# Who adds the squares at the fronts of stages, and where the low parts of twelve weight panels come from

## The chip, the cores and the metric

The kernel runs on one core of a Trainium2 chip. The metric is device time in microseconds (us), the median of the runs of one build. The engines are named PE (TensorE, matrix products), DVE (VectorE), ACT (ScalarE), POOL (GpSimd) and SP (SyncE, which issues most DMA transfers).

## What is computed

The reference is two blocks of a transformer in float32 on a sequence of 512 tokens and a width of 1024. Cut to what matters here:

```
def first_block(x, p, ...):
    for i in range(2):
        hn = rmsnorm(h, mix_norm[i])
        if i == 0: h = h + conformer_conv(hn, ...)
        else:      h = h + fox_attention(hn, ..., *shared_kv(h, kv_norm, ...))
        hn = rmsnorm(h, ffn_norm[i])
        h = h + square(relu(hn @ ffn_w1[i])) @ ffn_w2[i]
        gate = sigmoid(rmsnorm(h, ple_norm[i]) @ ple_w_gate[i])
        h = h + gate * (p[i] @ ple_w_proj[i])
    return rmsnorm(h, final_norm)

def second_block(x, mem, ...):
    h = rms_norm(x, mix_norm_gain)
    ... recurrence, block attention, memory attention, gated merge ...
    x = x + merged @ w_out
    h = rms_norm(x, ffn_norm_gain)
    x = x + (gelu(causal_dwconv(h @ w_ffn_gate, ...)) * (h @ w_ffn_up)) @ w_ffn_down
    return rms_norm(x, final_norm_gain)
```

Each `rmsnorm` divides by the root of the mean of squares over the 1024 features. Between the blocks two of them follow each other: the final norm of the first block and the first norm of the second.

## The kernel before

The hidden state `h` is held with features on the partitions: eight tiles of 128 features by 512 tokens. A float32 product is made of three passes on PE with operands rounded to a shorter type (fp32r): every operand is split in a high part, which is the rounded value, and a low part, which is the rest. Activations give `xh` and `xl`, weights `hi` and `lo`, and the passes are `xh*hi`, `xl*hi` and `xh*lo`, one 128x512 matmul each.

The weights come in panels of 128x2048 floats (1 MB), in the fixed order of a list of keys: `("w1", 1, 0, 0)` is the first panel of the first matrix of the second feed-forward layer, `("plg", l, i)` the gate of the per-layer part, `("xa", i)` the first panels of the second block. SP loads a panel into one of two `raw` buffers (`load`, line 299). `splitting` (line 529) then has ACT cast four pieces of 128x512 to `hi`, and DVE subtract them (`lo = raw - hi`, in `part`); panels of three kinds (`LO_POOL`, line 1901) have POOL subtract. Each piece of `hi` and `lo` has two buffers, so that a panel's piece takes the place of the same piece two panels before.

Panels in the set `SEVEN`, which are multiplied by a scheme of seven block products, get three of their low pieces in another way: `lows_by_dma` (line 367) has ACT write `-raw`, rounded, into `lo`, and POOL issue a DMA that reads the same weights from HBM again and adds them to that (line 362). Such a piece may begin when the panel before its own is the one being multiplied.

The order of all instructions is written by a planner, the class `Flow`. It keeps a clock per engine, from costs by operation, and a list of side jobs (generators); each time a matmul is written, the jobs that are due by these clocks take a step, by priority. So an instruction's place on its engine follows from costs and due times, and each engine then runs its own row in order.

A `Front` (line 687) makes the norm in front of a stage. As each of the eight tiles of `h` is finished, ACT writes its split `xh` and its square `sq`, and the squares are added up to one tile by `Norm.add` (line 639): the first square is the sum's start, six additions are POOL's and the last one DVE's. PE then takes the mean (four 1-column matmuls `tp<-C,sq`), DVE and POOL the inverse root, and PE spreads it (`tp<-C,s`). There are eight fronts. The first, at the program's start, uses two sums (`two=True`); the seven others are those before the feed-forward of the first layer (at about 244 us of the span), its per-layer gate (585), the second layer's mixing (633), its feed-forward (887) and its gate (1239), the second block (1286) and the second block's feed-forward (1735). At 1286 us a plain `Norm`, `n2` (line 1514), sums the squares for the final norm of the first block beside the front's own sum (`gg` in these rows is the product of gains by which `xh` is scaled there).

Of the kernel before, what the change touches and what calls it, by code (L numbers as in the profile page):

```python
# [15 lines left out]
S = 512  # L16
D = 1024
KT = 8
# [50 lines left out]
_KEYS = _panel_keys()  # L69
# [3 lines left out]
class Engine:  # L73


    def __init__(self, flow, eng, cost):
        self.flow, self.eng, self.cost, self.t, self.table = flow, eng, cost, 0.0, None
# [37 lines left out]
def _pe_cost(op, out, ins):  # L115
    n, dt = ins[1].free_size(), ins[1].dtype
    if op == "transpose" or (dt == F32 and n == 1):
        return 0.11
    if dt == F32:
        return 0.01 + n * 4 / 2400  # L120
    return max(0.109 if dt == F32R else 0.059, n / 2390)
# [106 lines left out]
def kernel(ctx: ExitStack, tc, gain0, x_t, p_t, mem_t, vec, w, w_f, w_lru, rows, consts, out):  # L228
# [9 lines left out]
    flow = Flow()  # L238
    act, dve = Engine(flow, nc.scalar, _act_cost), Engine(flow, nc.vector, _dve_cost)
    pool, pe = Engine(flow, nc.gpsimd, _pool_cost), Engine(flow, nc.tensor, lambda *a: 0.12 if flow.halves else _pe_cost(*a))  # L240
# [57 lines left out]
    raws, parts, early = {}, {}, {}  # L298

    def load(i, pieces=1):  # L300
        if i < len(_KEYS) and i not in raws:
            if _KEYS[i] in SEVEN:
                early[i] = flow.spawn(lows_by_dma(i), 0.0, 2)
            r = wp.tile([128, PW], F32, name=nm("raw"), tag="raw", bufs=2)
            raws[i] = r
            c = PW // pieces
            return [lambda k=k: dma(r[:, c * k:c * k + c], w[i, :, c * k:c * k + c]) for k in range(pieces)]
        return []

    class Panel:  # L310


        def __init__(self, key):
            self.key, self.blocked = key, key[0] in BLOCKED
            self.q = {}
# [24 lines left out]
    def part(i, k, pieces, low):  # L340

        if i not in parts:
            parts[i] = Panel(_KEYS[i])
        c = PW // pieces
        r = raws[i][:, c * k:c * k + c]
        hi, lo = parts[i].cols(c * k, c)
        gain = GAINED.get(_KEYS[i][0])
        if gain is not None:
            g = col(gain, k)
            act.activation(hi, r, AF.Copy, scale=g)  # L350
            dve.scalar_tensor_tensor(lo, r, g, hi.bitcast(F32), op0=ALU.mult, op1=ALU.subtract)
        else:
            act.copy(hi, r)
            low.tensor_sub(lo, r, hi.bitcast(F32))
# [12 lines left out]
    def lows_by_dma(i):  # L367

        r = raws[i]
        for b in range(3):  # L370
            c = slice(S * b, S * b + S)
            yield lambda: cur[0] >= i - 1 or (i - 2, b) in spent
            yield r[:, c]
            yield flow.quiet(act, patience=HOLD)
            if i not in parts:
                parts[i] = Panel(_KEYS[i])
            lo = parts[i].piece("lo", b)
            act.mul(lo, r[:, c], -1.0)
            yield lo
            accumulate(lo, w[i, :, c])  # L380

    def sums_split(i):
# [13 lines left out]
        pan.s1, pan.s2, pan.s3, pan.s4 = s1, s2, s3, s4  # L396
        wait = lambda e: flow.quiet(e, slack=1.2, patience=HOLD_SUMS)
        yield wait(dve)
# [130 lines left out]
    def splitting(i):  # L529
        if _KEYS[i] in SEVEN:  # L530
            yield from sums_split(i)
            return
        pieces = KT if _KEYS[i][0] in GAINED else 4
        low = pool if _KEYS[i][0] in LO_POOL else dve
        c = PW // pieces
        for k in range(pieces):
            yield raws[i][:, c * k:c * k + c]
            yield flow.quiet(act, low, patience=HOLD)
            part(i, k, pieces, low)

    ahead = {}
# [91 lines left out]
    class Norm:  # L633


        def __init__(self, n=S, total=KT, two=False):
            self.n, self.left, self.two = n, total, two
            self.parts = []

        def add(self, t, g=None):  # L640
            n = self.n
            self.left -= 1
            q = slot(p="sq")
            act.activation(q[:, :n], t, AF.Square, scale=1.0 if g is None else g)
            if len(self.parts) <= self.two:
                self.parts.append(q)
                return
            s = self.parts[self.left % (1 + self.two)]
            (dve if self.left % 2 and self.two or self.left == 0 else pool).tensor_add(s[:, :n], s[:, :n], q[:, :n])
            if self.left == 0 and self.two:  # L650
                dve.tensor_add(s[:, :n], s[:, :n], self.parts[1][:, :n])
            self.sum = s
# [31 lines left out]
    class Front:  # L684


        def __init__(self, g=None, two=False):
            self.g = g
            self.xs = [None] * KT
            self.norm = Norm(two=two)  # L690
            self.r4 = self.rbc = self.side = None

        def add(self, f, t):
# [861 lines left out]
    xa, ga = [None] * 4, [None] * 4  # L1555
# [311 lines left out]
    for n, cut, queues in zip(norms, cuts, ((dma,), (dma, nc.scalar.dma_start))):  # L1867
# [4 lines left out]
        s = flow.spawn(output(n, cut, queues), 0.0, 0)  # L1872
# [19 lines left out]
HOLD = 1.2  # L1892
# [7 lines left out]
MEM_PERIOD = 9.0  # L1900
LO_POOL = ("pw1", "vm", "o")
HOLD_SUMS = 0.3
BLOCKED = ("w1", "gu")
SEVEN = {("w1", l, c, i) for l in range(2) for c in range(1, 4) for i in range(4)}
SEVEN |= {("gu", m) for m in range(8, 24)}
# [156 lines left out]
```

## Time and profile before

| | us |
|---|---|
| median of three runs | 2131.7 |
| lowest and highest run | 2130.28 and 2131.87 |
| profiled execution, its own time | 2132.37 |
| its span on the core | 2129.5 |
| PE busy within the span | 2078.7 |

The span is the time from the first to the last instruction on the core, and 2.9 us lie around it. All windows and start times below count from the span's start. Of PE's 11360 matmuls most have 512 columns; at full clock they follow each other every 0.2265 us (six in a row start at 630.15, 630.37, 630.60, 630.83, 631.05 and 631.28 us). A matmul's own duration is longer than that, since matmuls are pipelined.

### The profile page before, as it was taken

What the parts mean: (1) busy time and instruction counts of PE and PEld (TensorE: products, weight loads), DVE (VectorE), ACT (ScalarE), POOL (GpSimd) and SP (SyncE); (2) the same over time, 40 slices, a digit from 0 to 9 for tenths busy, and PEclk for the clock granted to TensorE, in tenths of its full rate; (3) what the DMA queues carried; (4) which work ended last, traced back from release to release, by engine and by line L of the source; (5) the groups of instructions that cost most, each with busy time, mean ns of one, the idle gap of its engine ahead of it and who ended that gap; (6) DMA issues with size and microseconds to landing.
All of it is one profiled execution on the core that took longest, in us unless ns stands there. A gap on an engine that the chain in (4) does not pass through costs nothing.

```text
span 2129.5 us, 30406 instructions
## 1 busy us (share of the span) xinstructions
PE 2078.7 (98%) x11360; PEld 1783.7 (84%) x11360; DVE 1428.5 (67%) x2534; ACT 1159.2 (54%) x2372; POOL 473.2 (22%) x500
## 2 busy tenths in 40 slices
PE   7999999999999999899999999999999999999998
PEld 6867889899878887789898887878888888899997
DVE  5997557566576887666565677775574557776683
ACT  5776446456445676455464553665462333485672
POOL 4882101101121326401011121331010010020212
PEclk9999999999999999999999999999999999999999
DMA  5215236547322111236455523112222423375661
GB/s 185 99 61 197 88 115 155 129 129 183 115 81 86 61 62 61 70 106 142 125 153 127 170 87 123 62 61 101 99 71 88 139 80 119 112 158 147 148 170 60
DMA packets 58050, 240.73 MB, mean 113 GB/s; under 512 B 6824, under 2 KB 10152, under 8 KB 35504
## 3 DMA queue, kind: packets, MB, share of 16 engines
q1 hardware_dynamic: 40048, 206.81, 28.7%
q0 software_dynamic: 17280, 31.46, 9.1%
q8 instruction: 89, 1.46, 0.3%
q10 hardware_dynamic: 576, 0.52, 0.1%
q14 instruction: 57, 0.47, 0.1%
HBM read 229.00 MB, written 9.77 MB: 112 GB/s over the span
## 4 chain that ended last, share of the span: by engine, by line
PE 78%; DVE 10%; ACT 7%; issue 2%; POOL 2%; DMA 1%; SPq 0%; DVEq 0%; ACTq 0%; POOLq 0%
PE mm L83 69%; PE sc L83 6%; DVE t L83 2%; DVE sc L83 2%; ACT hi L83 2%; PE tp L83 1%; ACT t L83 1%; DVE lo L83 1%; PE ptp L83 1%; DVE xl L83 1%; POOL acc L83 1%; DVE h L83 1%; ACT lo L83 1%; DVE xc L83 1%; ACT sh L83 1%
## 5 line engine op out<-in xcount | busy, mean ns | idle before, releaser
L83 PE MATMUL mm<-xh,hi 128*128 128x512 f32 (+1 forms) x2096 | 797.6, 381 | 8.7 <-ACT hi L83 7.3
L83 PE MATMUL mm<-xh,lo 128*128 128x512 f32 (+1 forms) x2096 | 796.1, 380 | 7.0 <-DVE lo L83 6.6
L83 PE MATMUL mm<-xl,hi 128*128 128x512 f32 (+1 forms) x2096 | 795.4, 379 | 0.0
L83 PEld LDWEIGHTS mm<-xh,hi 128*128 128x128 f32 x2096 | 397.1, 189 | 79.6 <-ACT hi L83 7.6
L83 PEld LDWEIGHTS mm<-xh,lo 128*128 128x128 f32 x2096 | 396.8, 189 | 79.4 <-DVE lo L83 9.1
L83 PEld LDWEIGHTS mm<-xl,hi 128*128 128x128 f32 x2096 | 396.9, 189 | 69.5
L83 ACT CAST hi<-raw 128x512 fp32r<-128x512 f32 x596 | 347.2, 617 | 111.9 <-PE mm L83 96.3
L83 DVE TENSOR_TENSOR lo<-raw,hi 128x512 fp32r<-128x512 f32 x424 | 291.3, 724 | 60.5 <-ACT hi L83 58.6
L362 POOL DMA_DIRECT2D lo<-in_w x120 | 104.0, 866 | 760.5 <-ACT lo L83 699.5
L83 DVE TENSOR_TENSOR h<-mm,h 128x512 f32<-128x512 f32 (+1 forms) x113 | 75.5, 670 | 242.4 <-PE mm L83 242.3
L83 POOL TENSOR_TENSOR sq<-sq,sq 128x512 f32<-128x512 f32 (+1 forms) x69 | 84.5, 1226 | 437.2 <-ACT sq L83 436.6
L83 ACT ACTIVATE lo<-raw 128x512 fp32r<-128x512 f32 x120 | 76.5, 637 | 81.5 <-PE mm L83 81.5
L83 POOL TENSOR_SCALAR P<-P,s 128x128 f32<-128x128 f32 (+2 forms) x112 | 64.2, 578 | 243.4 <-DVE s L83 195.7
L83 DVE TENSOR_TENSOR sl<-sum,sh 128x512 fp32r<-128x512 f32 x120 | 82.4, 686 | 15.6 <-ACT sh L83 14.9
L83 PE MATMUL mm<-ch,sh 128*128 128x256 f32 x320 | 90.6, 283 | 0.0
L83 PE MATMUL mm<-cl,sh 128*128 128x256 f32 x320 | 90.6, 283 | 0.0
L83 PE MATMUL mm<-ch,sl 128*128 128x256 f32 x320 | 90.6, 283 | 0.0
L83 ACT ACTIVATE xh<-h,V 128x512 fp32r<-128x512 f32 x40 | 28.6, 722 | 112.9 <-DVE h L83 112.9
L83 PE MATMUL mm<-ch,hi 128*128 128x256 f32 x352 | 88.0, 285 | 1.6 <-ACT p L83 1.6
L83 ACT CAST sh<-sum 128x512 fp32r<-128x512 f32 x120 | 75.4, 628 | 20.1 <-DVE sum L83 20.1
L83 PE MATMUL mm<-ch,lo 128*128 128x256 f32 x288 | 81.5, 283 | 0.0
L83 POOL TENSOR_TENSOR acc<-acc,tap 128x482 f32<-128x482 f32 (+29 forms) x60 | 77.2, 1286 | 13.1 <-ACT tap L83 9.5
(295 smaller groups left out, 3908.1 us busy)
## 6 DMA issues: line engine op xcount, KB each, us to landing
raw<-in_w SPq DMA_DIRECT2D x175, 1024.0 KB
lo<-in_w POOLq DMA_DIRECT2D x120, 256.0 KB, 5.2
prd<-pr SPq DMA_DIRECT2D x16, 256.0 KB
pr<-prd SPq DMA_DIRECT2D x16, 256.0 KB
h<-in_x_t SPq DMA_DIRECT2D x8, 256.0 KB
resid<-h SPq DMA_DIRECT2D x8, 256.0 KB
h<-resid SPq DMA_DIRECT2D x8, 256.0 KB
out<-out SPq DMA_DIRECT2D x12, 128.0 KB
```

The source lines that it names most:

```text
L83: f(out, *args, **kw)
L362: nc.gpsimd.dma_start(out, src, accum_op=ALU.add)
```

## The change

Two things change. A `Norm` gets a flag `alone`, which all fronts but the first set: DVE then makes all seven additions of squares, so 42 additions go from POOL to DVE. `n2` has no such flag and keeps POOL. And a set `LO_DMA` names twelve panels, two of `w1` of the second layer, the two `xa` and the eight `plg`: their four low pieces come by `lows_by_dma`, ACT's negation and POOL's accumulating DMA, where DVE subtracted. `part` casts their high pieces only, and `splitting` waits for ACT alone there.

```
     def load(i, pieces=1):
         if i < len(_KEYS) and i not in raws:
-            if _KEYS[i] in SEVEN:
+            if _KEYS[i] in SEVEN or _KEYS[i] in LO_DMA:
                 early[i] = flow.spawn(lows_by_dma(i), 0.0, 2)
...
         c = PW // pieces
+        if _KEYS[i] in LO_DMA:
+            act.copy(parts[i].piece("hi", k), raws[i][:, c * k:c * k + c])
+            return
         r = raws[i][:, c * k:c * k + c]
...
     def lows_by_dma(i):
...
-        for b in range(3):
+        for b in range(3 if _KEYS[i] in SEVEN else 4):
...
-            yield flow.quiet(act, low, patience=HOLD)
+            yield flow.quiet(*((act,) if _KEYS[i] in LO_DMA else (act, low)), patience=HOLD)
...
-        def __init__(self, n=S, total=KT, two=False):
-            self.n, self.left, self.two = n, total, two
+        def __init__(self, n=S, total=KT, two=False, alone=False):
+            self.n, self.left, self.two, self.alone = n, total, two, alone
...
-            (dve if self.left % 2 and self.two or self.left == 0 else pool).tensor_add(s[:, :n], s[:, :n], q[:, :n])
+            (dve if self.alone or self.left % 2 and self.two or self.left == 0 else pool).tensor_add(
+                s[:, :n], s[:, :n], q[:, :n])
...
-            self.norm = Norm(two=two)
+            self.norm = Norm(two=two, alone=not two)
...
+LO_DMA = {("w1", 1, 0, 0), ("w1", 1, 0, 1), ("xa", 0), ("xa", 1)} | {("plg", l, i) for l in range(2) for i in range(4)}
```

The instructions of PE stay the same ones. Apart from the seven fronts and the twelve panels, each engine's row keeps its order, but for one load that SP issues earlier, ahead of eight transfers of the attention at about 650 us. What moves is shown at two places.

First ACT, at the front of the second feed-forward (the stretch from 878 to 890 us). `xh` and `sq` come from the eight tiles `h1755` to `h1762`, `raw1896` is panel `("w1", 1, 0, 0)`, `V_74` holds gains. Before:

```order
L83 ACTIVATE xh1921_9002<-h1755_8402,V_74 128x512
L83 ACTIVATE sq1927_9019<-h1755_8402 128x512
L83 ACTIVATE xh1923_9008<-h1756_8404,V_74 128x512
L83 ACTIVATE xh1925_9015<-h1757_8406,V_74 128x512
L83 ACTIVATE sq1933_9038<-h1756_8404 128x512
L83 CAST hi1937_9048<-raw1896_8872 128x512
L83 ACTIVATE xh1929_9027<-h1758_8408,V_74 128x512
L83 ACTIVATE xh1931_9034<-h1759_8410,V_74 128x512
L83 CAST hi1939_9060<-raw1896_8872 128x512
L83 ACTIVATE xh1935_9046<-h1760_8412,V_74 128x512
L83 ACTIVATE sq1941_9070<-h1757_8406 128x512
L83 CAST hi1945_9080<-raw1896_8872 128x512
```

and now:

```order
L83 ACTIVATE lo1921_8996<-raw1896_8888 128x512
L83 ACTIVATE lo1922_8999<-raw1896_8888 128x512
L83 ACTIVATE lo1923_9002<-raw1896_8888 128x512
L83 ACTIVATE lo1924_9005<-raw1896_8888 128x512
L83 ACTIVATE xh1925_9030<-h1755_8418,V_74 128x512
L83 ACTIVATE sq1931_9047<-h1755_8418 128x512
L83 ACTIVATE xh1927_9036<-h1756_8420,V_74 128x512
L83 ACTIVATE xh1929_9043<-h1757_8422,V_74 128x512
L83 ACTIVATE sq1937_9066<-h1756_8420 128x512
L83 CAST hi1941_9076<-raw1896_8888 128x512
L83 ACTIVATE xh1933_9055<-h1758_8424,V_74 128x512
L83 ACTIVATE xh1935_9062<-h1759_8426,V_74 128x512
```

The four negations of the panel stand ahead of the first `xh` of the front; behind them the casts and splits follow in the old order.

On DVE, at the same place, before (`raw1896` as above, `o`, `mm`, `sc` and `tp` results of PE):

```order
L83 SCALAR_TENSOR_TENSOR xl1926_9016<-h1757_8406,V_74,xh1925_9015 128x512
L83 TENSOR_TENSOR lo1938_9049<-raw1896_8872,hi1937_9048 128x512
L83 TENSOR_TENSOR lo1940_9061<-raw1896_8872,hi1939_9060 128x512
L83 SCALAR_TENSOR_TENSOR xl1930_9028<-h1758_8408,V_74,xh1929_9027 128x512
L83 SCALAR_TENSOR_TENSOR xl1932_9035<-h1759_8410,V_74,xh1931_9034 128x512
L83 TENSOR_TENSOR h1761_8414<-mm1934_9043,h1761_8414 128x512
L83 TENSOR_TENSOR lo1946_9081<-raw1896_8872,hi1945_9080 128x512
L83 SCALAR_TENSOR_TENSOR xl1936_9047<-h1760_8412,V_74,xh1935_9046 128x512
L83 TENSOR_TENSOR lo1949_9095<-raw1896_8872,hi1948_9094 128x512
L83 TENSOR_TENSOR h1762_8416<-mm1942_9076,h1762_8416 128x512
L83 SCALAR_TENSOR_TENSOR xl1944_9079<-h1761_8414,V_74,xh1943_9078 128x512
L83 TENSOR_TENSOR lo1959_9133<-raw1928_9024,hi1958_9132 128x512
```

and now:

```order
L83 SCALAR_TENSOR_TENSOR xl1930_9044<-h1757_8422,V_74,xh1929_9043 128x512
L83 SCALAR_TENSOR_TENSOR xl1934_9056<-h1758_8424,V_74,xh1933_9055 128x512
L83 TENSOR_TENSOR sq1931_9047<-sq1931_9047,sq1943_9093 128x512
L83 SCALAR_TENSOR_TENSOR xl1936_9063<-h1759_8426,V_74,xh1935_9062 128x512
L83 TENSOR_TENSOR h1761_8430<-mm1938_9071,h1761_8430 128x512
L83 TENSOR_TENSOR sq1931_9047<-sq1931_9047,sq1948_9112 128x512
L83 SCALAR_TENSOR_TENSOR xl1940_9075<-h1760_8428,V_74,xh1939_9074 128x512
L83 TENSOR_TENSOR sq1931_9047<-sq1931_9047,sq1950_9121 128x512
L83 TENSOR_TENSOR h1762_8432<-mm1944_9099,h1762_8432 128x512
L83 TENSOR_TENSOR sq1931_9047<-sq1931_9047,sq1956_9136 128x512
L83 SCALAR_TENSOR_TENSOR xl1946_9103<-h1761_8430,V_74,xh1945_9102 128x512
L83 TENSOR_TENSOR sq1931_9047<-sq1931_9047,sq1958_9151 128x512
```

The four `lo` subtractions of this panel are gone, and additions to the sum of squares `sq1931` stand between the splits; the tile `h1762` is taken up before four of them are done.

Second POOL, at the entry to the second block (1277 to 1288 us). `sq2602` (now `sq2609`) is the sum of `n2`, `sq2614` (now `sq2618`) the front's own. The last six additions on POOL before:

```order
L83 TENSOR_TENSOR sq2602_12621<-sq2602_12621,sq2644_12797 128x512
L83 TENSOR_TENSOR sq2614_12658<-sq2614_12658,sq2647_12812 128x512
L83 TENSOR_TENSOR sq2602_12621<-sq2602_12621,sq2650_12831 128x512
L83 TENSOR_TENSOR sq2614_12658<-sq2614_12658,sq2657_12851 128x512
L83 TENSOR_TENSOR sq2602_12621<-sq2602_12621,sq2668_12900 128x512
L83 TENSOR_TENSOR sq2614_12658<-sq2614_12658,sq2671_12915 128x512
```

and now, with the DMAs of the low pieces of the last `plg` and the `xa` panels:

```order
L83 TENSOR_TENSOR sq2609_12671<-sq2609_12671,sq2632_12776 128x512
L365 DMA lo2630_12769<-in_w 128x512
L83 TENSOR_TENSOR sq2609_12671<-sq2609_12671,sq2641_12823 128x512
L365 DMA lo2648_12846<-in_w 128x512
L365 DMA lo2649_12852<-in_w 128x512
L365 DMA lo2650_12858<-in_w 128x512
L365 DMA lo2651_12864<-in_w 128x512
L83 TENSOR_TENSOR sq2609_12671<-sq2609_12671,sq2655_12884 128x512
L83 TENSOR_TENSOR sq2609_12671<-sq2609_12671,sq2662_12926 128x512
L365 DMA lo2672_12954<-in_w 128x512
L365 DMA lo2673_12961<-in_w 128x512
```

The front's own additions are gone from POOL, and those of `n2` stand between the DMA issues. On DVE the last additions of that place were

```order
L83 TENSOR_TENSOR t2655_12846<-t2655_12846,pr2509_12160 128x512
L83 TENSOR_TENSOR h1761_8414<-h1761_8414,t2655_12846 128x512
L83 TENSOR_TENSOR t2662_12888<-mm2656_12848,rbc2595_12559 128x512
L83 SCALAR_TENSOR_TENSOR xl2670_12904<-h1761_8414,gg2578_12498,xh2669_12903 128x512
L83 TENSOR_TENSOR t2662_12888<-t2662_12888,pr2510_12162 128x512
L83 TENSOR_TENSOR h1762_8416<-h1762_8416,t2662_12888 128x512
L83 TENSOR_TENSOR lo2673_12928<-raw2642_12792,hi2672_12927 128x512
L83 TENSOR_TENSOR sq2602_12621<-sq2602_12621,sq2674_12933 128x512
L83 TENSOR_TENSOR lo2678_12944<-raw2642_12792,hi2677_12943 128x512
L83 SCALAR_TENSOR_TENSOR xl2676_12937<-h1762_8416,gg2578_12498,xh2675_12936 128x512
L83 TENSOR_TENSOR sq2614_12658<-sq2614_12658,sq2680_12956 128x512
```

and are now

```order
L83 TENSOR_TENSOR t2659_12898<-t2659_12898,pr2509_12184 128x512
L83 TENSOR_TENSOR h1761_8430<-h1761_8430,t2659_12898 128x512
L83 SCALAR_TENSOR_TENSOR xl2664_12930<-h1761_8430,gg2578_12526,xh2663_12929 128x512
L83 TENSOR_TENSOR sq2618_12706<-sq2618_12706,sq2665_12939 128x512
L83 TENSOR_TENSOR t2666_12942<-mm2660_12900,rbc2597_12595 128x512
L83 TENSOR_TENSOR t2666_12942<-t2666_12942,pr2510_12186 128x512
L83 TENSOR_TENSOR h1762_8432<-h1762_8432,t2666_12942 128x512
L83 TENSOR_TENSOR sq2609_12671<-sq2609_12671,sq2679_12993 128x512
L83 SCALAR_TENSOR_TENSOR xl2681_12997<-h1762_8432,gg2578_12526,xh2680_12996 128x512
L83 TENSOR_TENSOR sq2618_12706<-sq2618_12706,sq2684_13016 128x512
```

with no subtraction of a weight panel among them. PE's row has the means of these two sums at other places than before by a few matmuls: at 633 us the mean `tp<-C,sq` stands 8 matmuls later than before, at 887 us 6 later, and at 1286 us that of `n2` 4 later; the other fronts' stand where they stood.

## Rows read from the trace of the kernel before

**Rows 1.** The page: busy time of each engine, share of the span, instructions.

```profile
PE 2078.7 (98%) x11360; PEld 1783.7 (84%) x11360; DVE 1428.5 (67%) x2534; ACT 1159.2 (54%) x2372; POOL 473.2 (22%) x500
```

**Rows 2.** Waits of PE: line waited for, total us, times, longest.

```profile
PE tp L83 <- DVE sq L83: 13.3, 6, 4.2
...
PE mm L83 <- DVE lo L83: 6.6, 1, 6.6
```

**Rows 3.** Busy time by stretch (us) at the fronts, with granted clock and DMA share.

```profile
core 0: us, PE busy (x) PEld busy (x) DVE busy (x) ACT busy (x) POOL busy (x), PEclk, DMA share, GB/s
...
627.00:642.00 15.00, 13.11 (x66) 10.70 (x65) 10.55 (x20) 6.92 (x15) 3.42 (x3) 1.00 0.21 72
...
1281.00:1303.00 22.00, 17.97 (x83) 15.12 (x82) 13.80 (x24) 7.75 (x14) 4.63 (x4) 0.84 0.14 48
330.00:380.00 50.00, 50.00 (x380) 48.31 (x379) 36.30 (x69) 33.04 (x65) 5.72 (x7) 1.00 0.59 149
...
1259.00:1281.00 22.00, 22.00 (x99) 18.22 (x98) 18.70 (x22) 13.33 (x24) 10.70 (x8) 1.00 0.35 120
```

**Rows 4.** Timeline of PE around three stalls: start, us, instruction, [idle before <-releaser].

```profile
635.60 0.58 PE L83 MATMUL tp<-C,sq 128*128 128x1 f32 x4 [1.89 <-DVE sq L83]
...
894.38 0.80 PE L83 MATMUL mm<-xh,lo 128*128 128x512 f32 x1 [6.62 <-DVE lo L83]
...
897.54 0.45 PE L83 MATMUL mm<-xh,hi 128*128 128x512 f32 x1
...
1280.87 0.39 PE L83 MATMUL mm<-xh,lo 128*128 128x512 f32 x1
...
1290.73 1.84 PE L83 MATMUL tp<-C,sq 128*128 128x1 f32 x8 [4.03 <-DVE sq L83]
...
1296.84 1.03 PE L83 MATMUL tp<-C,sq 128*128 128x1 f32 x8
```

**Rows 5.** Timeline of ACT, DVE and POOL at 878 to 895 us.

```profile
878.56 0.72 ACT L83 ACTIVATE xh<-h,V 128x512 fp32r<-128x512 f32 x1 [8.59 <-DVE h L83]
...
886.30 0.61 ACT L83 CAST hi<-raw 128x512 fp32r<-128x512 f32 x1
...
885.86 3.45 DVE L83 SCALAR_TENSOR_TENSOR xl<-h,V,xh 128x512 fp32r<-128x512 f32 x2
...
892.58 1.74 DVE L83 TENSOR_TENSOR lo<-raw,hi 128x512 fp32r<-128x512 f32 x1
...
885.50 8.28 POOL L83 TENSOR_TENSOR sq<-sq,sq 128x512 f32<-128x512 f32 x5 [2.57 <-ACT sq L83]
```

**Rows 6.** Timeline of DVE and ACT at 1283 to 1291 us.

```profile
1283.80 0.69 DVE L83 TENSOR_TENSOR t<-mm,rbc 128x512 f32<-128x512 f32 x1
...
1286.56 1.75 DVE L83 TENSOR_TENSOR t<-t,pr 128x512 f32<-128x512 f32 x1
...
1289.07 0.72 ACT L83 ACTIVATE sq<-h,V 128x512 f32<-128x512 f32 x1 [2.26 <-DVE h L83]
```

**Rows 7.** Timeline of DVE and POOL at 629 to 636 us.

```profile
630.34 1.60 DVE L83 TENSOR_TENSOR t<-t,pr 128x512 f32<-128x512 f32 x1
...
634.77 0.68 DVE L83 TENSOR_TENSOR sq<-sq,sq 128x512 f32<-128x512 f32 x1
...
629.63 1.76 POOL L83 TENSOR_TENSOR sq<-sq,sq 128x512 f32<-128x512 f32 x1 [5.58 <-ACT sq L83]
```

**Rows 8.** Instructions on `lo` and `sq` tiles: count, ns min/median/max.

```profile
L83 ACT ACTIVATE lo<-raw x120: 625/632/672, 315.2 to 2056.4; 128x512 fp32r<-128x512 f32 x120
L362 POOL DMA_DIRECT2D lo<-in_w x120: 853/862/1053, 316.1 to 2057.5; - x120
...
L83 POOL TENSOR_TENSOR sq<-sq,sq x69: 727/1294/1837, 17.7 to 2117.3; 128x512 f32<-128x512 f32 x51, 128x256 f32<-128x256 f32 x18
```

**Rows 9.** DMA issues of the low pieces: count, KB, us to landing; whole program, then 330:380.

```profile
lo<-in_w POOLq DMA_DIRECT2D x120, 256.0 KB, 5.2
...
lo<-in_w POOLq DMA_DIRECT2D x7, 256.0 KB, 7.1
```

## The prediction, made before the changed kernel was run

> **What bounds the kernel now.** The page comes first: PE is busy 2078.7 of the 2129.5 us of the span, DVE, ACT and POOL for 67, 54 and 22% [rows 1]. PE is the bound, and any gain can only be time in which PE waits or runs at a lower clock. So the second view is the list of PE's waits, and in it the entries on the tiles that the change touches: sums of squares (six waits, 13.3 us) and low parts of weights (one wait, 6.6 us) [rows 2]. The timeline of PE puts them in place. Of the six waits for a sum, two stand at fronts that the change touches: 1.89 us before the mean that starts at 635.60, and 4.03 us before the one at 1290.73 [rows 4]. The other four, together 13.3 - 1.89 - 4.03 = 7.4 us, belong to the first front, the memory norm and the output, which keep their code. The wait for a low part, 6.62 us, ends at 894.38, in the first panel of the second feed-forward, which is one of the twelve. At the fronts at 244, 585, 1239 and 1735 us PE doesn't wait. So three places, 1.89 + 6.62 + 4.03 = 12.5 us, are in reach.
>
> The clock is read next. After the 1.89 us the granted clock stays 1.00, the 2.4 GHz level [rows 3]. After the two long waits it falls: in 1281:1303 it is 0.84 on the mean [rows 3], which is a stretch at 0.5 (1.2 GHz). The price is in PE's starts. From 894.38 to 897.54 there are 7 starts in 3.16 us [rows 4], at 0.2265 each they would take 1.59: 1.57 us lost. From 1290.73 to 1296.84 there are the four matmuls of a mean and ten others [rows 4]: 6.11 us where 4 x 0.22 + 10 x 0.2265 = 3.15 would do, 2.96 us lost.
>
> Last, who makes the three sums and the low part late. At all three places DVE works beside POOL's additions and takes long for them: 1.60 us for a product at 630.34, while POOL adds from 629.63 on [rows 7]; 3.45 us for two splits at 885.86 and 1.74 for the `lo` that PE waits for, while POOL adds for 8.28 us from 885.50 [rows 5]; 1.75 us at 1286.56 [rows 6]. Such operations without POOL beside them take 0.68 and 0.69 [rows 6, 7].
>
> **The change part by part.** *Engine time.* POOL loses 42 additions of 1.29 us, 54 us, and gets 48 DMA issues of 0.86 us, 41 us [rows 8]. DVE gets 42 additions and loses 48 subtractions, all about 0.68 [rows 7]: nearly even, 29 against 33 us. ACT gets 48 negations of 0.632 us, 30 us [rows 8]. PE gets and loses no instruction. Nothing of this counts by itself; it counts where PE waits.
>
> *Front at 633 us: -1.9 us.* The product ahead of the last tile no longer has POOL beside it (1.60 becomes 0.69, -0.9), one addition of 0.68 comes in front of it on DVE, and the mean stands 8 matmuls later, 8 x 0.2265 = 1.8 us. The sum was ready 1.89 us late; 1.8 + 0.9 - 0.7 = 2.0 us are made up. Bounds: 0.9 (if PE only gets the later place and DVE is 0.9 later with other work) and 2.0. I take 1.9, the whole wait, since the later place alone gives 1.8.
>
> *Front at 887 us: -6.9 us.* The `lo` that was waited for is now written by ACT and a DMA. Two things can be late in its place. One is the DMA: issue to landing is 5.2 us at the median and 7.1 in the busiest stretch [rows 9]. The other is ACT itself. The four negations stand ahead of the first `xh`, which starts at 878.56 after 8.59 us of idle time [rows 5]. If all four fit into that idle time, nothing moves; if none does, all that follows is 4 x 0.632 = 2.5 us later. The last of them must wait until PE has left the same piece of the panel two before, which by the order is late in that idle time, so I take 1.8 us of delay. The cast of the piece that PE needs for its fourth matmul here ended at 886.30 + 0.61 = 886.9 [rows 5]; it would end at 888.7, or 888.4 with a gap of 0.3 us on ACT that closes. The last low piece, issued at about 880.5, lands at 885.7 to 887.6, before that. PE came to wait at 894.38 - 6.62 = 887.8 by the end of its last matmul; its first matmul on the late cast is two starts earlier, so it will stand from about 887.2 to 888.4, some 1.3 us. Instead of 6.6 us it waits 1.3, and after so short a wait I expect no fall of the clock (there was none after 1.89 us): 5.3 + 1.6 = 6.9 us. Bounds: 8.2 (no delay on ACT) and 4 (the full 2.5 us and a slow stretch as before). Next late is the mean: it comes 6 matmuls later (1.4 us) and its sum has four additions of 0.68 on DVE behind the last tiles; I expect it just in time.
>
> *Second block, 1287 us: -6.6 us.* PE ends the product for the last tile at 1280.87 + 0.39 = 1281.3 [rows 4], but DVE takes it up only at 1283.80 [rows 6], after four subtractions of a panel that are now gone: up to 2.5 us. The product at 1286.56 takes 0.69 in place of 1.75, another 1.1. Against this ACT has four negations (2.5 us) in its row near the last square, which ACT awaited idle for 2.26 us [rows 6], so between 0 and 2.5 us is lost. The mean of `n2` stands 4 matmuls later, 0.9 us. Made up are 2.5 + 1.1 + 0.9 = 4.5 us less 0 to 2.5, against a wait of 4.03: a wait of 0 to 2.0 stays, and I take 0.4, near the low end, as the negations can run while DVE makes the last tile. Then the clock holds too: 3.6 + 3.0 = 6.6. Bounds 0 (below) and 7.0.
>
> *The other four fronts: 0.* The mean stands where it stood, PE didn't wait, and an addition on DVE takes 0.68 where POOL took 1.29. A negation ahead of the last `xh` could cost 0.6 at 585 and 1239 each; ACT is busy there for 13.33 of 22 us [rows 3], so I take none.
>
> *The twelve panels: 0.* A panel of 48 matmuls takes PE 10.9 us. The negations may start when the panel before begins; the first takes 0.63 us, its transfer lands up to 7.1 us after issue [rows 9], at 7.7; the fourth is issued behind three issues of 0.86 us [rows 8], at 3.2, lands at 10.3, and is wanted some 4 us into its panel. So the cover is 3 us for the first and 4 to 5 us for the fourth piece. What eats it is ACT's row: in 1259:1281 ACT would be busy 13.33 + 8 x 0.632 = 18.4 of 22 us [rows 3]. If the cover goes, each us late is a us of PE, on up to ten panels that follow at this pace. The 48 pieces add 12.6 MB of reads; with 0.59 of the DMA engines busy in 330:380, PE was busy for all 50 us there with pieces that come in this way [rows 3]. I take 0 and keep +2 for the range.
>
> POOL issues these DMAs while DVE is busy, and the trace shows such issues at 853 to 1053 ns, with DVE busy 36.30 of 50 us in 330:380 [rows 3, 8]. The Trainium skill, page "SBUF — State Buffer", section "SBUF: two separate sides", has a trap that speaks against it: descriptors of a DMA that POOL issues are starved while DVE runs an operation in a 2-port mode. By the trace 0 is paid for that, by the rule every issue could be held for the length of a DVE operation; the 120 issues don't bear it out.
>
> The sum: -1.9 - 6.9 - 6.6 = -15.4 us. Against the profiled execution's own time, 2132.4, it gives 2117.0; that execution is 0.7 above the median of 2131.7, which gives 2116.3. I predict 2117.
>
> **The rivals.** *A: the wait at 1287 us stays (chance 0.13).* POOL still adds for `n2`, now with DMA issues between, each of which waits for a negation on ACT. If these put the additions or the last square back by 3 us, 6.6 us are not gained: 2123. For it: ACT's row is fuller there; against: the last addition is DVE's, and POOL's row is nearly empty.
>
> *B: the wait at 887 us only changes its cause (0.11).* If ACT's last negation is held longer, or the last piece lands after 890, the wait is 3 to 4 us and the clock falls: some 2 us are gained there in place of 6.9, 2122.
>
> *C: the gains go again (0.08).* A and B together with some waits of 1 to 2 us at new places: 2128 to 2132.
>
> *D: slower (0.07).* The low pieces come late on the ten panels at the pace of 10.9 us. It decides at an issue-to-landing of 10.9 - 0.6 = 10.3 us for a first piece, or where ACT starts the negations 3 us late. If a piece has to wait for the transfers of another panel, 5.2 + 7.1 = 12.3 us, that is 2 us per panel: 2117 + 20 = 2137. Against it: PE waits for no low piece by DMA in the trace before [rows 2].
>
> *E: starved issues (0.02).* If DVE's operations held each issue by one contended operation of 1.75 us [rows 6], a panel's fourth piece would be 4 x 1.75 = 7 us later, 2.4 more than its cover, on ten panels: 2117 + 24 = 2141. This is the skill's trap of above; 120 issues of at most 1.05 us speak against it.
>
> **How the numbers follow.** My forecast has 0.59, A 0.13, B 0.11, C 0.08, D 0.07, E 0.02. With all bounds at their best the sum is -2.0 - 8.2 - 7.0 = -17.2, or 2114.5; with a us for the spread of runs the low end is 2113. The high end takes in A and B, the two cases next in chance, with a us or two of the panels' cover: 2125. 0.2% is 4.3 us, about what a measurement can tell from no change. Faster by more than that, under 2127.4, are my forecast, A and B: 0.83. C is the same, 0.08; D and E are slower, 0.09.
>
> **What would show it.** In the profile after, PE's waits should have no entry of 6 us for `lo`, one of about 1 us for `hi` near 887, none above 1 us for a sum at 633 and 1287, and the clock should be 1.00 in 886:901 and 1281:1303. DVE's splits at these places should take 0.7 us. The issue-to-landing of `lo` pieces should stay at 5 to 7 us. I would be wrong if PE waits for `lo` at the start of a `plg` or `xa` panel, if `xh` at 878 is more than 2 us later, or if POOL's issues get longer.

## The result, and the profile after

The changed kernel takes 2112.61 us (median of 5 runs, 2111.61 to 2114.20), the kernel before 2131.12 in the same comparison. The ratio is 0.9914, with a 95% interval of 0.9903 to 0.9925: 18.5 us less. I had said 2117 with 2113 to 2125 and a gain of 15.4. The direction and the three places were right, the time lies 0.4 us under the range.

The page of the changed kernel answers to [rows 1]: PE has lost 5.4 us of busy time (fewer of its matmuls run at the lower clock), DVE 28, POOL 17, ACT has gained 27.

```profile
PE 2073.3 (98%) x11360; PEld 1780.7 (84%) x11360; DVE 1400.6 (66%) x2528; ACT 1185.8 (56%) x2420; POOL 456.1 (22%) x506
```

The list of PE's waits answers to [rows 2]. The entry of 6.6 us on DVE's `lo` is gone. The sums have come down from 13.3 to 5.5 us, 5.3 of it at the fronts at 633 and 1287 and 2.5 at the first front, whose code is unchanged (4.21 us before, 1.75 now). A second wait for a cast (`hi`) has come in, 9.5 - 8.4 = 1.1 us; the 8.4 stand at the program's start.

```profile
PE mm L83 <- ACT hi L83: 9.5, 2, 8.4
PE tp L83 <- DVE sq L83: 5.5, 5, 1.8
PE ptp L83 <- DVE ptl L83: 2.5, 1, 2.5
```

The timeline of PE (start, us, instruction, idle before and its releaser) at the three fronts, for [rows 4]: at 631.73 the mean starts with no wait; at 884.10 PE has waited 1.12 us for the cast, where it waited 6.62 for `lo` (882.13 is its first matmul on that panel); 1269.22 is the last matmul of the product for the last tile of `h`, and at 1276.58 PE has waited 0.62 for the sum, where it was 4.03.

```profile
631.73 0.95 PE L83 MATMUL tp<-C,sq 128*128 128x1 f32 x8
...
882.13 0.39 PE L83 MATMUL mm<-xh,hi 128*128 128x512 f32 x1
...
884.10 0.50 PE L83 MATMUL mm<-xh,hi 128*128 128x512 f32 x1 [1.12 <-ACT hi L83]
...
1269.22 0.39 PE L83 MATMUL mm<-xh,lo 128*128 128x512 f32 x1
...
1276.58 1.02 PE L83 MATMUL tp<-C,sq 128*128 128x1 f32 x8 [0.62 <-DVE sq L83]
```

By stretch, for [rows 3], with the granted clock in the third column from the right. The fronts at 633, 887 and 1287 us of before lie in the first three rows now, all at 1.00 where the latter two had been slowed. The last row is a place of the second attention that the change doesn't touch: there the clock was below 1.00 in this trace and 1.00 in that of before.

```profile
core 0: us, PE busy (x) PEld busy (x) DVE busy (x) ACT busy (x) POOL busy (x), PEclk, DMA share, GB/s
618.00:633.00 15.00, 15.00 (x72) 12.57 (x71) 10.82 (x22) 7.58 (x17) 0.03 (x1) 1.00 0.21 71
875.00:890.00 15.00, 13.88 (x62) 11.16 (x61) 13.24 (x21) 14.42 (x27) 3.43 (x4) 1.00 0.44 108
1265.00:1287.00 22.00, 21.38 (x111) 17.84 (x110) 13.90 (x24) 13.21 (x26) 7.72 (x8) 1.00 0.74 172
820.00:832.00 12.00, 9.47 (x43) 7.81 (x43) 10.81 (x17) 4.94 (x12) 9.30 (x9) 0.86 0.00 0
```

ACT, DVE and POOL at the front of the second feed-forward, for [rows 5]. ACT's fourth negation waited 6.17 us for PE, and the first split starts right behind it; DVE makes two splits in 1.40 us where it took 3.45; POOL issues one DMA there, the fourth low piece's.

```profile
875.58 0.63 ACT L83 ACTIVATE lo<-raw 128x512 fp32r<-128x512 f32 x1 [6.17 <-PE sc L83]
876.12 0.71 ACT L83 ACTIVATE xh<-h,V 128x512 fp32r<-128x512 f32 x1
...
883.44 0.60 ACT L83 CAST hi<-raw 128x512 fp32r<-128x512 f32 x1
...
880.59 1.40 DVE L83 SCALAR_TENSOR_TENSOR xl<-h,V,xh 128x512 fp32r<-128x512 f32 x2
...
876.65 0.86 POOL L365 DMA_DIRECT2D lo<-in_w  x1 [5.38 <-ACT lo L83]
```

At the entry to the second block DVE's product ahead of the last tile, for [rows 6], takes 0.69 where it took 1.75:

```profile
1269.72 1.34 DVE L83 SCALAR_TENSOR_TENSOR xl<-h,gg,xh 128x512 fp32r<-128x512 f32 x1 [1.41 <-ACT xh L83]
1270.99 0.68 DVE L83 TENSOR_TENSOR sq<-sq,sq 128x512 f32<-128x512 f32 x1
1271.59 0.68 DVE L83 TENSOR_TENSOR t<-mm,rbc 128x512 f32<-128x512 f32 x1
1272.97 0.69 DVE L83 TENSOR_TENSOR t<-t,pr 128x512 f32<-128x512 f32 x1 [0.70 <-ACT t L83]
1273.69 0.69 DVE L83 TENSOR_TENSOR h<-h,t 128x512 f32<-128x512 f32 x1
1275.74 0.69 DVE L83 TENSOR_TENSOR sq<-sq,sq 128x512 f32<-128x512 f32 x1 [1.35 <-ACT sq L83]
```

And the DMA issues of the low pieces, for [rows 9], land after 5.4 us at the median, 168 of them where there were 120; the slowest took 10.9 us (issued at 1262.5), and PE waited for none:

```profile
lo<-in_w POOLq DMA_DIRECT2D x168, 256.0 KB, 5.4
```

**Where the 18 us are.** PE's row has the same number of instructions in both kernels, so the starts of the same matmul by number can be subtracted. The numbers leave out the one-column matmuls of the means, which stand at other places in the two rows, and 88 more between the 80th and the 2900th that are the same in both; the last row ends with the last matmul counted. The table gives the time that PE took from one such matmul to the next, in each profiled execution; the stretches named by a front hold that front.

| PE's matmuls | place | before | before again (e3) | changed | changed again (e4) |
|---|---|---|---|---|---|
| to 80 | start, code not changed | 37.28 | 33.83 | 34.26 | 34.77 |
| 80 to 2900 | | 566.35 | 566.32 | 565.74 | 565.66 |
| 2900 to 3080 | front at 633 | 43.09 | 44.57 | 40.95 | 40.94 |
| 3080 to 4150 | | 173.84 | 173.83 | 173.85 | 173.85 |
| 4150 to 4440 | end of an attention, not changed | 57.75 | 57.73 | 59.17 | 59.07 |
| 4440 to 4560 | front at 887 | 35.73 | 36.03 | 28.69 | 28.70 |
| 4560 to 6600 | | 355.27 | 355.31 | 355.00 | 355.00 |
| 6600 to 6760 | second block, 1287 | 43.52 | 43.70 | 37.20 | 37.20 |
| 6760 to the end | | 809.84 | 810.04 | 809.78 | 809.80 |

From the first trace of before to the first of after the fronts give -2.1, -7.0 and -6.3, together 15.5 us; the start gives -3.0, the attention +1.4, and -0.9 lies in small pieces, the largest of them 0.6.

### The profile page after: what moved, and what is told of

Read it like the earlier page. It is cut to its first block, busy times and chain, and to the rows that moved or that the text cites. A ratio compares the mean times of both kernels' runs of the same rounds, so it can differ in the third digit from the quotient of the medians.

```text
span 2111.4 us, 30465 instructions
## 1 busy us (share of the span) xinstructions
PE 2073.3 (98%) x11360; PEld 1780.7 (84%) x11360; DVE 1400.6 (66%) x2528; ACT 1185.8 (56%) x2420; POOL 456.1 (22%) x506
## 4 chain that ended last, share of the span: by engine, by line
PE 81%; DVE 8%; ACT 8%; issue 2%; POOL 1%; DMA 1%; SPq 0%; DVEq 0%; ACTq 0%; POOLq 0%
PE mm L83 72%; PE sc L83 6%; DVE sc L83 2%; ACT hi L83 2%; ACT t L83 1%; PE tp L83 1%; DVE t L83 1%; PE ptp L83 1%; ACT lo L83 1%; DVE xc L83 1%; ACT xh L83 1%; ACT sh L83 1%; POOL acc L83 1%; DMA h<-in_x_t 1%; ACT sq L83 0%
## 5 line engine op out<-in xcount | busy, mean ns | idle before, releaser
L83 PE MATMUL mm<-xh,hi 128*128 128x512 f32 (+1 forms) x2096 | 796.3, 380 | 10.9 <-ACT hi L83 9.5
L365 POOL DMA_DIRECT2D lo<-in_w x168 | 147.0, 905 | 912.0 <-ACT lo L83 846.4
L83 DVE TENSOR_TENSOR lo<-raw,hi 128x512 fp32r<-128x512 f32 x376 | 245.6, 692 | 46.8 <-ACT hi L83 44.5
L83 ACT ACTIVATE lo<-raw 128x512 fp32r<-128x512 f32 x168 | 105.4, 633 | 103.7 <-PE mm L83 95.6
L83 POOL TENSOR_TENSOR acc<-acc,tap 128x482 f32<-128x482 f32 (+29 forms) x60 | 77.3, 1288 | 13.1 <-ACT tap L83 9.5
L83 DVE SCALAR_TENSOR_TENSOR sc<-u,V,sc 128x511 f32<-128x511 f32 (+21 forms) x116 | 78.8, 731 | 0.5
L83 POOL TENSOR_TENSOR lo<-raw,hi 128x512 fp32r<-128x512 f32 x52 | 69.5, 1360 | 38.7 <-ACT hi L83 38.5
```

Of the source, the lines that this page charges most:

```text
L83: f(out, *args, **kw)
L365: nc.gpsimd.dma_start(out, src, accum_op=ALU.add)
```

## The experiments

Each kernel is timed against the kernel before in the same comparison, whose median was 2130.3 to 2131.1 us; several have a time of 2112 to 2116, so the stretches of the table above are what tells them apart.

**e1: the additions alone.** The set of panels is empty:

```
-LO_DMA = {("w1", 1, 0, 0), ("w1", 1, 0, 1), ("xa", 0), ("xa", 1)} | {("plg", l, i) ...}
+LO_DMA = set()
```

> DVE adds the squares at the seven fronts, but the twelve panels' low parts stay DVE's subtractions (the set LO_DMA is empty). Theory 1 (what makes PE wait at the three fronts is DVE slowed by POOL's additions, and DVE's row being too full at 887 and 1287): the wait at 633 goes (-2), at 887 the wait for lo falls from 6.6 to about 4 with the slow clock still there (-2.5), at 1287 from 4.0 to about 2 (-2 to -5): about 2123. Rival (POOL beside DVE is the whole cause): all of the gain of the three fronts, 15 us, comes from this part alone: about 2116, and the low parts by DMA add nothing.

Measured: 2114.86 us, ratio 0.9932 (0.9919 to 0.9946). The three fronts take 40.94, 29.64 and 38.35 us: -2.1, -6.1 and -5.2 against the first trace of before, 13.4 of the 15.5 us. The rival came much nearer than my theory. By its time alone e1 can't be told from the changed kernel (2112.61, and 2114.14 in e4 below); the stretches tell them apart. PE still waits for `lo` at 887, for 2.09 us; DVE's row there now has splits of 0.75 and subtractions of 0.69 us with the additions between them, where [rows 5] had 1.7 each:

```profile
884.20 0.50 PE L83 MATMUL mm<-xh,lo 128*128 128x512 f32 x1 [2.09 <-DVE lo L83]
...
880.39 0.69 DVE L83 TENSOR_TENSOR sq<-sq,sq 128x512 f32<-128x512 f32 x1
880.99 0.75 DVE L83 SCALAR_TENSOR_TENSOR xl<-h,V,xh 128x512 fp32r<-128x512 f32 x1
881.65 0.69 DVE L83 TENSOR_TENSOR h<-mm,h 128x512 f32<-128x512 f32 x1
882.25 0.69 DVE L83 TENSOR_TENSOR lo<-raw,hi 128x512 fp32r<-128x512 f32 x1
882.85 0.69 DVE L83 TENSOR_TENSOR sq<-sq,sq 128x512 f32<-128x512 f32 x1
883.45 0.69 DVE L83 TENSOR_TENSOR lo<-raw,hi 128x512 fp32r<-128x512 f32 x1
```

The page of e1 shows the same for the whole program: DVE makes 42 additions more, some 29 us at 0.69, and is busy for 1429.9 us where it was 1428.5 [rows 1]. So its other instructions take some 27 us less than beside POOL's additions.

```profile
PE 2071.6 (98%) x11360; PEld 1778.3 (84%) x11360; DVE 1429.9 (68%) x2576; ACT 1159.2 (55%) x2372; POOL 414.3 (20%) x458
```

A part of e1's gain has another cause. The planner writes the means later on PE's row: by 8 matmuls at 633, and by 15 at the second block, which is 3.4 us at 0.2265 each and more than the 4 of the changed kernel. There the sum is ready 7.2 us after PE's last product of `h`, where it was 9.3 before. So 2.1 of the 4.03 us of wait go because the sum is earlier; the other 1.9 are covered by the later place of the mean, for which PE doesn't wait:

```profile
1278.22 0.95 PE L83 MATMUL tp<-C,sq 128*128 128x1 f32 x8
```

At 633 the sum is 1.3 us earlier, and the later place covers the last 0.6. At 887 the wait was for `lo`, which a later mean doesn't shorten; but the sum behind it would now come 1.1 us late at the old place, 8 matmuls earlier.

**e2: the low parts alone.** The fronts' additions stay on POOL:

```
-            self.norm = Norm(two=two, alone=not two)
+            self.norm = Norm(two=two)
```

> The twelve panels' low parts come by negation and accumulating DMA, the squares at the fronts are added by POOL as before. Theory 1: at 887 PE waits about 1.3 us for a cast of ACT in place of 6.6 for lo (-7), at 1287 the product for the last tile is taken up 2.5 us earlier but the sum is still late by 1 to 2 us (-2 to -5), at 633 0 to -1: about 2120. Rival (POOL beside DVE is the whole cause): DVE's splits at 885 to 892 keep taking 1.7 us each, and the gain stays under 5 us: 2126 or more.

Measured: 2124.47 us, ratio 0.9967 (0.9957 to 0.9977). The fronts take 41.59, 32.36 and 45.27 us: -1.5, -3.4 and +1.8. At 887 the wait for `lo` has become 1.1 us for a cast, as I had said, but 1.1 for the sum come behind it, and a slow clock. At the second block it got worse: PE waits 0.65 us for a low piece, whose DMA was issued at 1259.17 behind an addition of POOL, with its negation done at 1256.28, and took 8.2 us to land; it waits 3.00 for the sum, and the clock is at 0.5 for 10 us. PE first, then DVE at the front at 887, where single splits next to POOL's additions still take up to 1.5:

```profile
1267.43 0.50 PE L83 MATMUL mm<-xh,lo 128*128 128x512 f32 x1 [0.65 <-DMA lo<-in_w]
...
1282.06 1.39 PE L83 MATMUL tp<-C,sq 128*128 128x1 f32 x8 [3.00 <-DVE sq L83]
...
882.86 1.45 DVE L83 SCALAR_TENSOR_TENSOR xl<-h,V,xh 128x512 fp32r<-128x512 f32 x1
...
886.20 1.52 DVE L83 SCALAR_TENSOR_TENSOR xl<-h,V,xh 128x512 fp32r<-128x512 f32 x1 [0.19 <-ACT xh L83]
```

So 13.4 us come from the additions alone and 3.1 from the low parts alone, against 15.5 for both. Each part has its own places, and the low parts at the second block pay only once POOL's additions are away.

**e3 and e4: both kernels again, for second traces.** No edit.

> The kernel before, unchanged, for a second trace. The changed kernel gained 3.0 us in the first 40 us of the span, where its instructions are those of before. Theory 1: that part is set by when the input tiles land, and is no effect of the change: this trace reaches PE's 80th instruction at another time than 37.3 us, by 1 us or more, or the second trace of the changed kernel does. Rival: the start belongs to the change; then this trace shows 37.3 again within 0.3 us, with a wait of 4.2 us for the first sum. Time 2131.

> The changed kernel, unchanged, for a second trace. Theory 1: the three fronts show the same waits as in its first trace (0 at 633, 1.1 for a cast at about 884, 0.6 for a sum at about 1275) and the start and the stretch of attention at 820 to 830 us, where the first trace had a granted clock of 0.5 for 3.4 us, may differ. Rival: the start is again 34.3 us at PE's 80th instruction, within 0.3 us, and so belongs to the change. Time 2112.6.

Measured: 2131.13 us (ratio 1.0004, 0.9995 to 1.0013) and 2114.14 (0.9925, 0.9911 to 0.9938). The start of the kernel before took 37.28 us in one trace and 33.83 in the other, with a wait for the first sum of 4.21 and 2.54 us, so it isn't the change's. PE in the trace of before at the start:

```profile
24.67 1.86 PE L83 MATMUL tp<-C,sq 128*128 128x1 f32 x8 [4.21 <-DVE sq L83]
```

PE in e3 at the start and at the front at 633, and that front's stretch:

```profile
23.35 1.05 PE L83 MATMUL tp<-C,sq 128*128 128x1 f32 x8 [2.54 <-DVE sq L83]
...
632.12 1.02 PE L83 MATMUL tp<-C,sq 128*128 128x1 f32 x8 [1.89 <-DVE sq L83]
...
634.04 0.63 PE L83 MATMUL mm<-xl,hi 128*128 128x512 f32 x1
634.47 0.63 PE L83 MATMUL mm<-xh,lo 128*128 128x512 f32 x1
```

```profile
627.00:642.00 15.00, 13.12 (x60) 10.80 (x59) 8.70 (x17) 5.67 (x14) 2.57 (x3) 0.89 0.23 81
```

In e3 the wait at 633 is again 1.89 us, but this time matmuls behind it start 0.43 us apart and the granted clock of 627:642 is 0.89, where [rows 3] had 1.00. The same wait costs 1.89 us or 3.4, by the run.

**e5 and e6: one group of panels each, with the additions on DVE.**

```
e5: LO_DMA = {("xa", 0), ("xa", 1)} | {("plg", l, i) for l in range(2) for i in range(4)}
e6: LO_DMA = {("w1", 1, 0, 0), ("w1", 1, 0, 1)}
```

> The changed kernel, but the two w1 panels' low parts stay DVE's subtractions; plg and xa come by DMA. Theory 2 (after the first runs: DVE's additions without POOL beside it make nearly the whole gain, and each low part by DMA only what is left of its own front): the stretch at 887 is as with the additions alone (a wait of 2.1 us for lo, 29.6 us from PE's matmul 4440 to 4560), the entry to the second block as in the changed kernel (a wait of 0.6 for the sum, 37.2 us from matmul 6600 to 6760): about 2114.5. Rival (the low parts help each other, for instance through POOL's or ACT's row): one of the two stretches differs by over 1 us from these values. The lower clock at 826 us of the changed kernel, seen in both of its traces, 1.4 us: theory 2 has it as chance, not bound to these panels.

> The changed kernel, but only the two w1 panels' low parts come by DMA. Theory 2: the stretch at 887 is as in the changed kernel (1.1 us of wait for a cast, 28.7 us from matmul 4440 to 4560), the entry to the second block as with the additions alone (38.35 us, waits of 0.8 for POOL and 0.7 for DVE after the mean): about 2113.5. Rival: as above, a stretch off by over 1 us.

Measured: 2115.70 us (ratio 0.9930, 0.9915 to 0.9944) and 2113.32 (0.9920, 0.9904 to 0.9937). e5 has 29.65 at 887 and 37.17 at the second block, e6 28.72 and 38.35: of these two fronts each group of panels moves its own and not the other, to 0.05 us. The two `w1` panels are worth 0.95 us, the ten others 1.15.

**e12: six additions of seven left out.** From e1, six of the seven additions of squares at the seven fronts are left out, on either engine:

```
                 self.parts.append(q)
                 return
+            if self.alone and self.left:
+                return
             s = self.parts[self.left % (1 + self.two)]
```

> As e1_adds_only, but six of the seven additions of squares at the seven fronts are left out altogether (the sum is the first square and the last). It asks what the additions cost on DVE, when POOL has none. Theory 2 (the additions fit into DVE's idle time, and what was gained is that POOL no longer works beside DVE): the three stretches are those of e1_adds_only within 0.5 us (40.9, 29.6 and 38.35), about 2114.5. Rival (DVE's row is full at the fronts, and the additions hold back splits and low parts): the wait of 2.1 us for lo at 882 shrinks by the two or three additions ahead of it on DVE, 1.4 to 2 us, and the entry to the second block by up to 1: about 2112.

Measured: 2112.59 us, ratio 0.9919 (0.9903 to 0.9936). The fronts take 40.94, 28.53 and 36.41 us: against e1 0.0, -1.1 and -1.9. The means stand where they stood in the kernel before, and PE waits for none of the three: without these additions the sums are in time at the old places. DVE has as many instructions as in the kernel before, 2534, and they take 1403.9 us where they took 1428.5 beside POOL's additions. The rival holds at two fronts: on DVE the additions do cost something, 3.0 us, where DVE also subtracts low parts. With the low parts gone by DMA, as in the changed kernel, 28.69 and 37.20 are left: at 887 that is as good as with the six left out.

**e7, e8 and e9: what is left.** On the changed kernel, the first front adds on DVE alone too (e7); `w1(1,0,0)` has its fourth low piece subtracted by DVE, so that no negation waits for PE (e8); `n2` adds on DVE (e9).

```
e7: -            self.norm = Norm(two=two, alone=not two)
    +            self.norm = Norm(two=two, alone=True)
e8: -        for b in range(3 if _KEYS[i] in SEVEN else 4):
    +        for b in range(3 if _KEYS[i] in SEVEN or _KEYS[i] == ("w1", 1, 0, 0) else 4):
    -        if _KEYS[i] in LO_DMA:
    +        if _KEYS[i] in LO_DMA and (_KEYS[i], k) != (("w1", 1, 0, 0), 3):
e9: -    n2 = Norm()
    +    n2 = Norm(alone=True)
```

> The changed kernel with the additions of the first front too on DVE alone; before, DVE and POOL add there side by side, DVE's additions take 1.4 to 1.8 us and PE waits 1.8 to 4.2 us for the sum. Theory 2: seven additions at 0.6 us follow the squares, the sum is ready about 3 us earlier, the wait goes, and so does some of the time at the lower clock: -2 to -4, about 2110. Rival (the first front waits for the landing of the input tiles, or POOL's subtractions of the next panel hold DVE in its additions' place): no gain within 1 us.

> The changed kernel, but of panel w1(1,0,0) three low pieces come by DMA and DVE subtracts the fourth, so that ACT has no negation that awaits PE ahead of the front's first split. Theory 2: the splits start 0.6 us earlier (876.1 becomes 875.5), the cast that PE waits for ends 0.6 us earlier, but the fourth piece's subtraction follows that cast on DVE: the wait of 1.1 us for the cast becomes 0.5 for the cast and up to 1 for lo. Time 2112 to 2113.5, no clear gain. Rival (ACT's row is the whole wait): the wait goes, -1.3 us.

> The changed kernel with the additions of n2 at the entry to the second block on DVE too, so that POOL adds no square there. Theory 2 (POOL's additions count only where DVE or the sum is late): the wait of 0.6 us for the sum goes, since DVE's product ahead of the last square no longer meets POOL: -0.6 to -0.8 in that stretch, 36.4 in place of 37.2. Rival: six more additions on DVE put the last tile back by as much: 37.2 or more.

Measured: e7 2110.48 us (ratio 0.9906, 0.9891 to 0.9921), its start 31.68 us against 34.26 and 34.77, with no wait for the first sum. e8 2112.62 (0.9917, 0.9902 to 0.9932), the front at 887 27.85 against 28.69: PE's wait there is 0.3 us for `lo`. e9 2112.38 (0.9915, 0.9900 to 0.9929), the second block 36.35 against 37.20 and no wait in it. The theories held in the stretches of e7 and e9. That of e8 left 0.5 us of wait for the cast and up to 1 for `lo`; 0.3 are left, so e8 lies between its theory and its rival. Of the times alone only e7's lies clearly under that of the changed kernel.

**e10 and e11: all three together**, with the ten other panels by DMA (e10) or by DVE (e11, `LO_DMA` as in e6).

> The changed kernel with all three edits of this round and the last: the first front and n2 add on DVE, and w1(1,0,0) has three low pieces by DMA and the fourth by DVE. Theory 2: the gains add up: -2.6 at the start, -0.85 at 887, -0.7 at 1287, about 2109.

> As e10_best, but plg and xa stay with DVE's subtractions, so that only seven pieces come by DMA. Theory 2: the entry to the second block has DVE's subtractions again, 1 to 2 us more than e10_best there (waits of 0.7 to 0.8 after the mean); the stretch of the second attention lacks the slow clock that followed the wait at 822 us with these panels (1.4 us) if that is bound to them: 2108 to 2110. Rival (that slow clock is chance): about 2110.5.

Measured: e10 2107.32 us, ratio 0.9891 (0.9876 to 0.9906); e11 2110.24, 0.9904 (0.9888 to 0.9921). In e10 the stretches are 31.73, 27.85 and 36.35: the gains add up, and it beats both kernels. In e11 the second block is at 38.35 again. The lower clock behind the wait at about 822 us is there in e11, which has no `plg` or `xa` panel by DMA, and was not there in e2, which has all of them: these panels alone don't make it. That it is chance isn't shown either. All seven traces with the fronts' additions on DVE and the ten panels by DMA have it (after, e4, e5, e7 to e10), of the seven others e11 alone; no row here says why. If it belongs to the two together, the changed kernel pays 1.4 us there for the 2.1 that the panels gain at the fronts.

The list of PE's waits in e10 has one entry from 870 to 900 us:

```profile
PE mm L83 <- DVE lo L83: 0.3, 1, 0.3
```

It has none from 1265 to 1300.

## Why the prediction was right and where it was wrong

**The bound, the three places, the four fronts and the panels: right.** Only PE's waits and its clock counted. The fronts at 244, 585, 1239 and 1735 gained and lost nothing above the small pieces of the table, and PE waited for no low piece by DMA in the changed kernel, though ACT was busy in 14.42 of 15 us at 887 and one piece took 10.9 us to land where I had said 5 to 7.

**The sizes of the fronts: right within 0.3 us.** -1.9, -6.9 and -6.6 were forecast, -2.1, -7.0 and -6.3 measured. At 887 the delay of ACT was put at 1.8 us: in the kernel before, the first split started 7.91 us ahead of PE's first matmul on this panel (878.56 and 886.47), now 6.0 us (876.12 and 882.13), for the reason given: the fourth negation waited for PE. So was the wait that took the place, 1.3 forecast and 1.12 shown by the trace; at the second block 0.4 was forecast and 0.62 came.

At the second block the size came out by luck, for its terms didn't. I gave up to 2.5 us to DVE's earlier start on the product for the last tile. Before, DVE took it up 2.54 us after PE's last matmul on it (1281.26 to 1283.80), now 1.98 (1269.61 to 1271.59): 0.6 us earlier, since a split and an addition stand in the place of the subtractions. The product beside POOL gave 1.06 of the 1.1 forecast. Another 1.4 us, which I didn't have, came from a split that stood between DVE's two steps on the last tile and now stands ahead of them; ACT's casts ahead of the last square took 0.5 back. The sum is 2.5 us earlier by this, and the later mean gives the forecast 0.9. DVE and POOL there in the kernel before:

```profile
1285.29 1.34 DVE L83 SCALAR_TENSOR_TENSOR xl<-h,gg,xh 128x512 fp32r<-128x512 f32 x1 [0.80 <-ACT xh L83]
1286.56 1.75 DVE L83 TENSOR_TENSOR t<-t,pr 128x512 f32<-128x512 f32 x1
...
1286.44 1.31 POOL L83 TENSOR_TENSOR sq<-sq,sq 128x512 f32<-128x512 f32 x1 [0.36 <-ACT sq L83]
```

**What made them: wrong at 887 and 1287.** The step that failed is the reading of which half of the change pays. I put the 6.9 us at 887 down to the `lo` that comes by ACT and a DMA, and the largest term at 1287, 2.5 us, to the subtractions that leave DVE. e1 shows that the additions alone give 6.1 and 5.2 there (at 1287 in part by the later mean), e2 that the low parts alone give 3.4 and -1.8. The trace of before had it: in [rows 5], 3.45 us for two splits and 1.74 for the `lo` are 3.1 us more than the 1.40 + 0.69 that these three take without POOL, and more such operations stood in the same queue. I named this slowness as the cause of the stalls and then priced its end for one product at 633 and one at 1287 alone (0.9 and 1.1 us), and not at 887. It shows in DVE's busy time too, which I had as nearly even, 29 us more and 33 less: it fell by 28. The Trainium skill, page "SBUF — State Buffer", section "Who interferes with whom", says that a DVE instruction with two inputs in SBUF contends with a GpSimd instruction that reads SBUF, and that the later of the two waits. These traces agree: such an instruction takes 0.69 or 0.75 us alone and 1.5 to 1.75 beside POOL, and in the lines above DVE's product, which starts just after POOL's addition, ends 0.56 us after it, while the addition takes the 1.3 us that it takes alone.

**What the additions cost on DVE: put at nothing beyond 0.7 us at 633, and that holds for the front at 887 of the changed kernel.** e12 prices them at 1.1 and 1.9 us where DVE also has the low parts. This is what the low parts by DMA buy back (0.95 and 1.15 us, e5 and e6), about a fifth of the 6.9 + 2.5 that I gave them.

**The range: the term for unchanged places was mis-sized.** I gave a us for the spread of runs. The start alone took 37.28 us in the trace that I summed from, 33.83 in the next one of the same kernel, 33.9 to 35.1 in nine others with the same start (the changed kernel, e1, e2, e4, e5, e6, e8, e9, e12): I summed against an execution with a late start, and the gain of 3.0 there isn't the change's. And after waits of nearly the same length the clock fell in some executions and not in others: at 633, in one of the two traces of before; at about 822 us, in an attention whose code is unchanged, in 8 of 14 traces, behind waits of 2.5 to 2.6 us, while the longest two there, 2.67 (before) and 2.90 (e12), had no fall behind them. My sentence that it holds after 1.89 us rested on one trace. With the start and the clock as they may fall, 2112 was well within reach of the same sum, and the low end should have been near 2111, my best case of 2114.5 less the 3.4 us between the two starts of before. By how little the range was missed is luck: the same kernel took 2114.14 us in its second comparison (e4), inside the range, and its gain there was 16.1.

**The rivals.** A and B didn't come, nor C. D, late low pieces, showed once, in e2: 0.65 us for one piece, whose issue stood behind an addition on POOL. E: no row shows an issue of POOL held by DVE. Some records of issues got longer, up to 1.55 us, but these overlap: three that stand one behind the other take 2.72 us, 0.91 each, with DVE idle for the 7.14 us ahead of 873.49. POOL and DVE of the changed kernel there:

```profile
868.55 2.72 POOL L365 DMA_DIRECT2D lo<-in_w  x3 [3.12 <-ACT lo L83]
...
873.49 0.69 DVE L83 TENSOR_TENSOR h<-mm,h 128x512 f32<-128x512 f32 x1 [7.14 <-PE mm L83]
```

## What to carry to other kernels

When two engines are both late at one place, ask first whether one makes the other slow: a row that takes 1.7 us for what takes 0.7 elsewhere is a cause with a price of its own, and moving the small work that disturbs can be worth more than taking away the large work that is waited for. Where a change has two halves, price each of them alone. And for a range, compare two traces of the same kernel: what differs between them in places that the change doesn't touch is the least width that a range can have.

## What the runs showed of the hardware that I had not expected

The granted clock after a wait isn't a function of the wait's length alone: 1.89 us at the same place of the same program was followed by a stretch at 0.5 in one execution (e3) and not in the other, which makes the same wait cost 1.9 or 3.4 us. At about 822 us a wait of 2.53 us was followed by a fall in the changed kernel and by none in e1, e2 and e6.
